# Modulation vectors summed along the free axis, a first mixer input built chunk by chunk, and angle tables moved into the first MLP

## The chip, the cores and the metric

The kernel runs on one core of one Trainium2 chip. A core has five engines with a queue each: PE (TensorE, matmuls), DVE (VectorE), ACT (ScalarE), POOL (GpSimd) and SP (SyncE, which here issues nearly all DMAs). Tensors live in SBUF with 128 partitions; PE sums into PSUM, eight banks of 128x512 fp32. The metric is the device time of one execution in microseconds (us), the median of several; lower is better.

## What is computed

Two stacks of two layers each over 512 tokens of width 1024, in fp32. A layer of the first stack is two sandwiches, a mixer and an MLP. Each has a modulation of its own, worked out from one vector c:

```python
def sandwich(x, c_act, sublayer, g_pre, g_post, w_mod, b_mod):
    shift, scale, gate = jnp.split(c_act @ w_mod + b_mod, 3, axis=-1)
    h = rms_norm(x, g_pre) * (1 + scale[:, None]) + shift[:, None]
    return x + gate[:, None] * rms_norm(sublayer(h), g_post)

def first_block(x, c, ...):
    c_act = jax.nn.silu(c)
    for layer in range(2):
        mixer = even_mixer if layer % 2 == 0 else odd_mixer
        x = sandwich(x, c_act, mixer, ...)
        x = sandwich(x, c_act, squared_relu_mlp, ...)
    return x
```

So there are 2 x 2 x 3 = 12 modulation vectors of 1024 numbers, each a product of c_act with a 1024x1024 matrix (4 MB). The even mixer (layer 0) projects `h` to the queries, keys and values of eight differential attention heads and to the inputs of a state-space part (SSD); the odd mixer (layer 1) is a retention beside a windowed attention. The second stack has gated delta, sparse and stick-breaking attention, a convolutional FFN, and an embedding added to the residual as `h + gate * rmsnorm(p[i] @ w_ple[i], ple_norm[i])`. Its rotary attention needs cosines and sines of `positions * inv`.

## The kernel before, in words

Activations stand transposed: eight chunks `x[k]` of 128 channels by 512 tokens. The kernel is written with a tile framework: the program gives the order of work, and a scheduler orders each engine's queue by the program's order (`high_priority(400)` moves a block ahead) and puts in the waits.

A projection's fp32 weights come in units of 128x1024 (512 KB). `wunit` (line 400) loads one (`wraw`, three buffers `wr`), rounds it on ACT into `whi` (`L409`), and takes the rest `wlo` on DVE (`L411`), or on GpSimd with `side=True`; `whi` and `wlo` have three buffers each. The activations are split likewise into `hh` and `hl`. `mm3` does three matmuls (hi by hi, lo by hi, hi by lo: `L418` to `L420`), 512 columns each, for every 128x128 block. `fm` gives outputs with features on partitions; `tm` (lines 452 to 466) gives tokens on partitions, in two passes of 256 columns (`L463` to `L465`), and is used for the values. `lead` starts two units at once, in the PSUM banks `s`.

Modulation: a step (`mod_step`, line 567) loads 128 rows of a matrix, multiplies them by 128 numbers of c_act, one to a partition, and adds to an accumulator (`mod_add`, `L583` and `L585`, 128x1024). After eight steps `mod_end` sums over the partitions by eight fp32 matmuls with a column of ones (`L592`; each is two records in the trace), and adds the bias. The steps of later vectors stand in a queue `modq`: `wunit` takes one per weight unit, unless `hold` says to let some units pass first.

The start (line 1943 on): the angle tables (`rope_tables`, two sines with two switches of ACT's function table), the loads of x, c_act from eight columns (`setup_c`), the statistic of x (`x_rstd`, eight squares `L332` on ACT, eight fp32 matmuls `L321`). `first_mod` makes the first two vectors, in halves of 512 outputs: five of eight row blocks go through PE with the column of c_act as the stationary side (`L619`), three through DVE. `pre_mod` then scales the eight chunks and splits them; for the first mixer its products `x[k] * r` are on GpSimd (`L657`). `even_mixer` begins with `diff_attention`: the leads of the first head's query and key units, and then, for each two heads, two value units by `tm` and the queries, keys, scores, softmax and values of the heads. `L802` is the scores' bias and row minimum in one pass, `L813` and `L817` are the transposes and the product with the values. The SSD part follows, then the output projection.

A statistic `Stat` squares on ACT (`L332`) and sums on PE (`L321`); with `side` set, the first `side` squares are summed on GpSimd (`L334`) and go to PE as one. `post_mod_` (line 666) normalises and adds to the residual (`L672`, `L673`, then the split `L482`); `ple_values` (line 1885) projects the embeddings of a layer, with its rests and its statistic on GpSimd, and stands at the end of MLP 0 and of the odd mixer.

Of the kernel before, what the change touches and what calls it, by code (L numbers as in the profile page):

```python
# [14 lines left out]
T = 512  # L15
# [20 lines left out]
def _tm_units(w):  # L36

    k, f = w.shape
    w = w.reshape(2, 4, 128, f // 256, 256).transpose(3, 0, 2, 1, 4)
    return np.ascontiguousarray(w.reshape(-1, 128, 1024))  # L40
# [146 lines left out]
def layout(inp):  # L187
# [4 lines left out]
    mw = g["mod_w"].reshape(4, 8, 128, 3, 1024).transpose(0, 3, 1, 2, 4)  # L192
# [3 lines left out]
    a["e_v"] = _tm_units(w[:, V:V + 1024])  # L196
# [58 lines left out]
    v.append(("c", _cols(g["c"][0])))  # L255
# [86 lines left out]
class Build:  # L342
# [218 lines left out]
    def setup_c(self):  # L561
        nc = self.nc
        self.cact = self.vp.tile([128, 8], F32, name="cact")
        e = self.sigmoid(self.vp, self.V("c"), tag="csg")
        nc.vector.tensor_mul(self.cact, e, self.V("c"))

    def mod_step(self, l, s, part, k):


        nc = self.nc  # L570
        if k == 0:
            self.macc = self.vp.tile([128, 1024], F32, tag="macc", name="macc", bufs=1)
        w = self.wr.tile([128, 1024], F32, tag="wr", name="mw")
        nc.sync.dma_start(w, self.ins["modw"][((l * 2 + s) * 3 + part) * 8 + k])
        self.mod_add(self.macc, w, k)
        if k == 7:
            self.mods[l, s, part] = self.mod_end(l, s, part, self.macc, slice(0, 8))

    def mod_add(self, acc, w, k, c=None):
        c = k if c is None else c  # L580
        col = self.cact[:, c:c + 1]
        if k == 0:
            self.nc.vector.tensor_scalar(acc, w, col, None, MUL)  # L583
        else:
            self.nc.vector.scalar_tensor_tensor(acc, w, col, acc, MUL, ADD)  # L585

    def mod_end(self, l, s, part, acc, ks):
        nc = self.nc
        ps = self.bank("t")
        n = ks.stop - ks.start  # L590
# [11 lines left out]
    def first_mod(self, pool):  # L602

        nc = self.nc
        ms = {}
        n = 512
        for i in range(2):
            for part in (1, 0):
                acc = pool.tile([128, n], F32, tag="macc", name="macc", bufs=4)
                ps = self.bank("d")  # L610
                first = [True, True]
                for k in range(8):
                    w = pool.tile([128, n], F32, tag="mw", name="mw", bufs=28)
                    nc.sync.dma_start(w, self.ins["modw"][8 * part + k][:, n * i:n * i + n])
                    if k in (2,4,6,):
                        self.mod_add(acc, w, 0 if first[1] else k, k)
                        first[1] = False
                    else:
                        nc.tensor.matmul(ps[0:1, 0:n], self.cact[:, k:k + 1], w, start=first[0], stop=False)  # L619
                        first[0] = False  # L620
                nc.tensor.matmul(ps[0:1, 0:n], self.C("ones")[:, 0:1], acc, start=False, stop=True)
                row = pool.tile([1, n], F32, tag="mrow", name="mrow", bufs=2)
                nc.vector.tensor_copy(row, ps[0:1, 0:n])
# [1309 lines left out]
def program(tc, ins, out, vat, phases=("mix0", "mlp0", "mix1", "mlp1", "b0", "b1", "fin")):  # L1933
    with ExitStack() as ctx:
# [3 lines left out]
        with ExitStack() as c1:  # L1938
# [6 lines left out]
            if first:  # L1945
                b.setup_c()
# [58 lines left out]
```

## Time and profile before

| | us |
|---|---|
| median of 3 runs | 3418.83 |
| lowest, highest | 3412.20, 3424.08 |
| the profiled execution | 3426.16 |
| its span (first to last instruction) | 3424.4 |
| PE busy in it | 3280.0 |
| DVE, ACT, POOL busy | 2216.6, 1690.6, 294.3 |
| mean granted TensorE clock | 0.982 of full speed |

A profile is one execution taken by the hardware profiler. A row of it gives the line of the program, the engine, the operation, and what is written from what. Matmuls are pipelined, so the busy times of neighbouring ones overlap; the distance from start to start is what one costs in a full stream. A wait is put down to the instruction that released it.

### The profile page before, as it was taken

The numbers are of one execution on the slowest core, as the hardware profiler recorded it, in microseconds if no ns is written. First come the engines' busy times: TensorE is split into PE (matmuls) and PEld (weight loads), VectorE is DVE, ScalarE is ACT, GpSimd is POOL, SyncE is SP. The second block draws the span as 40 slices with busy tenths as digits, with TensorE's granted clock in tenths as the row PEclk, the third lists the DMA queues.
The fourth block names the chain that finished last, engine by engine and source line by source line (L and its number), as shares of the span: only waits on it lengthen the run. The fifth ranks groups of instructions, "written<-read, shape, count | busy, mean of one in ns | idle before, by whom it ended". The sixth has DMA issues, their size and how long they took to land. (4 is left out here: it accounts for less than half of the span.)

```text
span 3424.4 us, 45576 instructions
## 1 busy us (share of the span) xinstructions
PE 3280.0 (96%) x17752; PEld 2580.1 (75%) x17752; DVE 2216.6 (65%) x3650; ACT 1690.6 (49%) x2922; POOL 294.3 (9%) x204
## 2 busy tenths in 40 slices
PE   8999998999989998999899999999989999999997
PEld 4877775888768776888667777888877777788885
DVE  6678775544486555444566766776776776587676
ACT  4666554323374335222355657544455565654445
POOL 2000111000110012000201002000030110200002
PEclk9999999999999999999989999999999999999998
DMA  7343222532333442232221002322322100222322
GB/s 260 117 146 116 68 74 73 172 113 93 106 108 117 148 136 95 93 98 93 83 74 62 26 31 77 99 96 95 99 89 75 62 26 22 80 96 95 99 93 77
DMA packets 97112, 323.93 MB, mean 95 GB/s; under 512 B 10936, under 2 KB 12472, under 8 KB 96768
## 3 DMA queue, kind: packets, MB, share of 16 engines
q1 hardware_dynamic: 96160, 319.44, 28.5%
q8 instruction: 140, 2.29, 0.3%
q10 hardware_dynamic: 576, 1.05, 0.1%
q14 instruction: 76, 0.62, 0.1%
q0 software_dynamic: 160, 0.52, 0.0%
HBM read 313.61 MB, written 9.98 MB: 94 GB/s over the span
## 5 line engine op out<-in xcount | busy, mean ns | idle before, releaser
L409 ACT CAST whi<-wr 128x1024 fp32r<-128x1024 f32 x459 | 480.3, 1048 | 867.1 <-PE pss L419 421.7
L411 DVE TENSOR_TENSOR wlo<-wr,whi 128x1024 fp32r<-128x1024 f32 x409 | 501.6, 1228 | 373.3 <-ACT whi L409 371.2
L418 PE MATMUL psg<-hh,whi 128*128 128x512 f32 x1448 | 584.3, 404 | 7.7 <-DVE gu L837 7.4
L420 PE MATMUL psg<-hh,wlo 128*128 128x512 f32 x1448 | 577.0, 398 | 0.0
L419 PE MATMUL psg<-hl,whi 128*128 128x512 f32 x1448 | 576.6, 398 | 0.0
L418 PE MATMUL pss<-hh,whi 128*128 128x512 f32 x784 | 310.6, 399 | 30.9 <-ACT hh L475 11.1
L418 PEld LDWEIGHTS psg<-hh,whi 128*128 128x128 f32 x1448 | 274.4, 190 | 67.1 <-issue 6.4
L420 PEld LDWEIGHTS psg<-hh,wlo 128*128 128x128 f32 x1448 | 273.4, 189 | 58.7 <-issue 5.8
L419 PEld LDWEIGHTS psg<-hl,whi 128*128 128x128 f32 x1448 | 273.7, 189 | 57.7 <-issue 7.4
L419 PE MATMUL pss<-hl,whi 128*128 128x512 f32 x784 | 312.3, 398 | 3.2 <-DVE hl L482 3.2
L420 PE MATMUL pss<-hh,wlo 128*128 128x512 f32 x784 | 311.0, 397 | 0.0
L334 POOL TENSOR_TENSOR sqacc<-sqacc,sq 128x512 f32<-128x512 f32 x86 | 126.5, 1471 | 1690.7 <-ACT sq L332 1689.9
L418 PE MATMUL psg<-mh,whi 128*128 128x512 f32 x560 | 223.9, 400 | 1.4 <-DVE x L680 1.3
L420 PE MATMUL psg<-mh,wlo 128*128 128x512 f32 x560 | 220.7, 395 | 0.0
L419 PE MATMUL psg<-ml,whi 128*128 128x512 f32 x560 | 220.1, 394 | 0.0
L418 PEld LDWEIGHTS pss<-hh,whi 128*128 128x128 f32 x784 | 150.2, 192 | 70.0 <-ACT hh L475 15.7
L419 PEld LDWEIGHTS pss<-hl,whi 128*128 128x128 f32 x784 | 151.1, 193 | 38.0 <-DVE hl L482 4.6
L420 PEld LDWEIGHTS pss<-hh,wlo 128*128 128x128 f32 x784 | 150.8, 192 | 34.0 <-issue 2.0
L411 POOL TENSOR_TENSOR wlo<-wr,whi 128x1024 fp32r<-128x1024 f32 x50 | 122.6, 2452 | 616.4 <-ACT whi L409 593.7
L418 PE MATMUL pss<-mh,whi 128*128 128x512 f32 x432 | 171.1, 396 | 0.5 <-DVE x L680 0.5
L420 PE MATMUL pss<-mh,wlo 128*128 128x512 f32 x432 | 169.7, 393 | 0.0
L419 PE MATMUL pss<-ml,whi 128*128 128x512 f32 x432 | 169.6, 392 | 0.0
(628 smaller groups left out, 6318.3 us busy)
## 6 DMA issues: line engine op xcount, KB each, us to landing
wr<-w SPq DMA_DIRECT2D x128, 512.0 KB, 3.5
wr<-up SPq DMA_DIRECT2D x88, 512.0 KB, 3.5
mw<-modw SPq DMA_DIRECT2D x80, 512.0 KB, 3.5
wr<-in SPq DMA_DIRECT2D x48, 512.0 KB, 3.5
wr<-down SPq DMA_DIRECT2D x40, 512.0 KB, 3.4
wr<-e_ssd SPq DMA_DIRECT2D x24, 512.0 KB, 3.5
wr<-e_qk SPq DMA_DIRECT2D x16, 512.0 KB, 4.1
mw<-modw SPq DMA_DIRECT2D x32, 256.0 KB, 5.4
```

The lines of the kernel that those rows point to most:

```text
L334: nc.gpsimd.tensor_add(self.acc, self.acc, sq)
L409: self.nc.scalar.copy(hi, raw)
L411: eng.tensor_sub(lo, raw, hi.bitcast(F32))
L418: mm(ps, ws[0], xs[0], start=first, stop=False)
L419: mm(ps, ws[0], xs[1], start=False, stop=False)
L420: mm(ps, ws[1], xs[0], start=False, stop=last)
```

## The change

The first mixer's input and its values are made chunk by chunk in `first_chunks`. Each of the eight channel chunks k takes its own 128 outputs of the scale and of the shift: the modulation weights are stored transposed, outputs on partitions, and `tensor_tensor_reduce` multiplies a 128x1024 tile by c_act (now a row of 1024, the same on all partitions) and sums along the row, starting at the bias, into one column. The chunk is scaled and split, and its 24 matmuls of the value projection go at once into all eight PSUM banks, 512 columns each. The value units are stored for that in another order (`_tw_units`); `diff_attention` copies the finished values out at its start and has neither value units nor leads. All other modulation vectors are summed in the same way, with no matmul and no accumulator. The angle tables are made in MLP 0 after the third group's first half, in the buffers `pt` of its activations. Three statistics that were summed on GpSimd are summed on PE (both embeddings' and the one after MLP 1), and the embeddings' rests are taken on DVE. The first mixer's products `x[k] * r` go from GpSimd to DVE, and `hold` is 12 there instead of 4.

```diff
     def mod_step(self, l, s, part, k):
         if k == 0:
-            self.macc = self.vp.tile([128, 1024], F32, tag="macc", name="macc", bufs=1)
+            self.mcol = self.vp.tile([128, 8], F32, name=f"mod{l}{s}{part}")
         w = self.wr.tile([128, 1024], F32, tag="wr", name="mw")
         nc.sync.dma_start(w, self.ins["modw"][((l * 2 + s) * 3 + part) * 8 + k])
-        self.mod_add(self.macc, w, k)
+        self.mod_dot(l, s, part, k, w, self.mcol[:, k:k + 1])
...
+    def mod_dot(self, l, s, part, k, w, col):
+        b = 8 * part + k
+        self.nc.vector.tensor_tensor_reduce(w, w, self.cact, 1.0, self.V(f"mb{l}{s}")[:, b:b + 1], MUL, ADD, col)
...
-        for j in range(n):
-            nc.tensor.matmul(ps[:, j:j + 1], acc[:, 128 * j:128 * j + 128], self.C("ones")[0:acc.shape[0], :1], start=True, stop=True)
-        m = self.vp.tile([128, n], F32, name=f"mod{l}{s}{part}{ks.start}")
-        nc.vector.tensor_add(m, ps[:, :n], self.V(f"mb{l}{s}")[:, 8 * part + ks.start:8 * part + ks.stop])
...
+    def setup_c(self, pool):
+        self.cact = self.vp.tile([128, D], F32, name="cact")
+        nc.sync.dma_start(self.cact, self.ins["crow"].to_broadcast([128, D]))
+        e = self.sigmoid(pool, self.cact, tag="mw", bufs=14)
+        nc.vector.tensor_mul(self.cact, e, self.cact)
...
+    def first_chunks(self, pool):
+        r = self.first_rstd
+        self.hold = 12
+        hs, ws = [], {}
+        acc = [[self.pg.tile([128, T], F32, tag="g", name="psg") if b < 2 and u == 0 else
+                self.bank("ggdd"[b] if u == 0 else "ssto"[b]) for b in range(4)] for u in range(2)]
+        for k in range(KC):
+            if k % 2 == 0:
+                ws = [self.wunit("e_v", k + u, 2) for u in range(2)]
+            cols = []
+            for part in (1, 0):
+                w = pool.tile([128, D], F32, tag="mw", name="mw", bufs=14)
+                nc.sync.dma_start(w, self.ins["modw"][8 * part + k])
+                m = self.vp.tile([128, 1], F32, name=f"mod00{part}{k}")
+                self.mod_dot(0, 0, part, k, w, m)
+                cols.append(self.mod_end(0, 0, part, m, slice(k, k + 1)))
+            t = self.nb.tile([128, T], F32, tag="pt", name="pt", bufs=3)
+            nc.vector.tensor_mul(t, self.x[k], r)
+            nc.scalar.activation(t, t, ACTF.Identity, scale=cols[0], bias=cols[1])
+            h = self.split(self.hp, "h", t)
+            hs.append(h)
+            for (hi, lo), pss in zip(ws, acc):
+                for b, ps in enumerate(pss):
+                    s = slice(128 * b, 128 * b + 128)
+                    mm = nc.tensor.matmul
+                    mm(ps, h[0][:, s], hi[:, k % 2], start=k == 0, stop=False)
+                    mm(ps, h[0][:, s], lo[:, k % 2], start=False, stop=False)
+                    mm(ps, h[1][:, s], hi[:, k % 2], start=False, stop=k == KC - 1)
+        return hs, acc
...
     def post_mod_(self, y, st, g, name):
-        self.xstat = Stat(self, KC, 7 if name else 0)
+        self.xstat = Stat(self, KC)
...
     def mlp(self, l, hs):
+                if g == 2 and l == 0:
+                    self.rope_tables()
...
     def diff_attention(self, hs, acc, p, outs):
+        v = p.tile([128, 4, D], F32, name="v")
+        for u in range(2):
+            for b in range(4):
+                nc.scalar.copy(v[:, b, T * u:T * u + T], acc[u][b])
-        self.lead("e_qk", (0, 1), hs)
         for u in range(4):
-            v = p.tile([128, 4, 256], F32, tag="v", name="v", bufs=2)
-            for b, ps in self.tm("e_v", u, hs):
-                nc.scalar.copy(v[:, 2 * b:2 * b + 2], ps)
...
     def ple_split(self, l, p):
-            self.nc.gpsimd.tensor_sub(lo, pt[:, k], hi.bitcast(F32))
+            self.nc.vector.tensor_sub(lo, pt[:, k], hi.bitcast(F32))
...
     def ple_values(self, l, p, hs):
-        st = Stat(self, KC, KC, tag="o", pool=p)
+        st = Stat(self, KC, tag="o", pool=p)
-            for j, ps in self.fm(f"ple_{l}", u, hs, side=True):
+            for j, ps in self.fm(f"ple_{l}", u, hs):
...
-            b.rope_tables()
-            b.load_x()
-            b.setup_c()
-            b.first_rstd = b.x_rstd(True)
...
                         with b.scope("mod0") as pm:
-                            b.first_mod(pm)
+                            b.setup_c(pm)
+                            b.load_x()
                             b.t5_tables()
-                            hs = b.pre_mod(0, 0, pm)
+                            b.first_rstd = b.x_rstd(True)
+                            hs, acc = b.first_chunks(pm)
```

## Rows read from the trace of the kernel before

**Rows 1.** Page, part 1: each engine's busy us, share of span, instructions

```profile
PE 3280.0 (96%) x17752; PEld 2580.1 (75%) x17752; DVE 2216.6 (65%) x3650; ACT 1690.6 (49%) x2922; POOL 294.3 (9%) x204
```

**Rows 2.** Windows: busy us of PE, PEld, DVE, ACT, POOL; clock; DMA; GB/s

```profile
0.00:10.00 10.00, 1.32 (x2) 0.81 (x3) 3.71 (x18) 4.00 (x8) 0.20 (x4) 1.00 0.67 227
10.00:20.00 10.00, 9.45 (x18) 3.42 (x18) 4.22 (x10) 9.10 (x13) 1.35 (x3) 1.00 1.05 361
```

**Rows 3.** Groups, 0-60 us: xcount | busy us, mean ns | idle before, releasers

```profile
L619 PE MATMUL psd<-mw,cact 128*1 128x512 f32 x40 | 19.9, 607 | 1.0 <-DMA mw<-modw 1.0
L418 PE MATMUL pss<-hh,whi 128*128 128x512 f32 x11 | 4.2, 412 | 0.0
L332 ACT ACTIVATE sq<-x 128x512 f32<-128x512 f32 x8 | 4.8, 625 | 3.3 <-DMA x<-xT 2.4 <-PE pst L321 0.8
```

**Rows 4.** Timeline of the start: start us, us, engine, line, operation [idle before]

```profile
23.21 0.68 DVE L532 SCALAR_TENSOR_TENSOR ry<-ry 128x512 f32<-128x512 f32 x1
40.26 1.52 ACT L658 ACTIVATE pt<-pt,mod,mod 128x512 f32<-128x512 f32 x2 [16.73 <-DVE mod L594]
```

**Rows 5.** Timeline, PE: first and last of two unbroken runs, narrow and wide

```profile
65.66 0.28 PE L465 MATMUL psg<-whi,hl 128*128 128x256 f32 x1
...
68.90 0.28 PE L465 MATMUL psg<-whi,hl 128*128 128x256 f32 x1
...
222.26 0.39 PE L418 MATMUL psg<-hh,whi 128*128 128x512 f32 x1
...
234.30 0.39 PE L420 MATMUL psg<-hh,wlo 128*128 128x512 f32 x1
```

**Rows 6.** Groups, 60-290 us, DVE; the last is a group of the page

```profile
L411 DVE TENSOR_TENSOR wlo<-wr,whi 128x1024 fp32r<-128x1024 f32 x27 | 33.0, 1222 | 26.5 <-ACT whi L409 26.4
L585 DVE SCALAR_TENSOR_TENSOR macc<-mw,cact,macc 128x1024 f32<-128x1024 f32 x22 | 28.2, 1280 | 5.5 <-DMA mw<-modw 5.4
L802 DVE CUSTOM_DVE_ANT_0 l<-pss,tt 128x512 f32<-128x512 f32 x16 | 10.9, 688 | 1.7 <-PE pss L519 0.8 <-PE psd L813 0.6
L802 DVE DVE_READ_ACCUMULATOR2_ANT sm<- 128x1 f32 x64 | 5.3, 83 | 0.0
L409 ACT CAST whi<-wr 128x1024 fp32r<-128x1024 f32 x459 | 480.3, 1048 | 867.1 <-PE pss L419 421.7
```

**Rows 7.** Windows of the attention, the SSD's beginning and MLP 0

```profile
60.00:270.00 210.00, 204.49 (x1186) 169.88 (x1186) 151.99 (x355) 136.35 (x291) 0.00 (x0) 1.00 0.42 135
290.00:350.00 60.00, 58.24 (x297) 44.82 (x296) 50.21 (x77) 32.35 (x51) 6.60 (x3) 1.00 0.46 148
600.00:940.00 340.00, 339.58 (x1481) 274.25 (x1479) 166.30 (x192) 105.68 (x135) 14.61 (x9) 1.00 0.37 120
```

**Rows 8.** Timeline, PE: one modulation vector's sixteen column products, and what follows

```profile
151.55 1.84 PE L592 MATMUL pst<-const,macc 128*128 128x1 f32 x16
153.25 0.36 PE L463 MATMUL psg<-whi,hh 128*128 128x256 f32 x1
```

**Rows 9.** Timeline, PE: first scores of two heads in succession

```profile
234.66 0.39 PE L518 MATMUL pss<-kt,qt 128*128 128x256 f32 x1
...
251.27 0.39 PE L518 MATMUL pss<-kt,qt 128*128 128x256 f32 x1 [0.40 <-ACT kt L508]
```

**Rows 10.** Post-modulation of MLP 0: a DVE group, and the window

```profile
L673 DVE SCALAR_TENSOR_TENSOR x<-y,mod,x 128x512 f32<-128x512 f32 x8 | 9.8, 1260 | 0.0
944.00:973.00 29.00, 18.54 (x50) 9.49 (x49) 23.04 (x25) 17.20 (x30) 12.61 (x8) 0.84 0.29 106
```

**Rows 11.** The same group in the odd mixer (1290 to 1316 us)

```profile
L672 DVE TENSOR_TENSOR y<-y,ry 128x512 f32<-128x512 f32 x8 | 10.5, 1356 | 0.0
```

**Rows 12.** Timeline after MLP 1, DVE, while GpSimd is idle

```profile
1685.97 1.29 DVE L672 TENSOR_TENSOR y<-y,ry 128x512 f32<-128x512 f32 x2
1687.19 1.41 DVE L673 SCALAR_TENSOR_TENSOR x<-y,mod,x 128x512 f32<-128x512 f32 x2
```

**Rows 13.** Waits of PE: us in total, times, longest us

```profile
PE pso L321 <- POOL sqacc L334: 8.5, 2, 4.5
```

More of the change, by code (lines that the diff above doesn't have):

```diff
@@ L600, in mod_end @@
         return m
-    def first_mod(self, pool):
+    def first_chunks(self, pool):
         nc = self.nc
-        ms = {}
-        n = 512
-        for i in range(2):
-            for part in (1, 0):
[L609 to L623, printed above, removed]
-                ms[part, i] = self.mod_end(0, 0, part, row, slice(n // 128 * i, n // 128 * (i + 1)))
-        for part in range(2):
-            self.mods[0, 0, part] = [ms[part, i] for i in range(2)]
@@ L655, in pre_mod_ @@
         for k in range(KC):
-            t = pool.tile([128, T], F32, tag="pt", name="pt", bufs=bufs)
-            mul.tensor_mul(t, self.x[k], r)
-            nc.scalar.activation(t, t, ACTF.Identity, scale=at(a, k), bias=at(shift, k))
+            t = self.nb.tile([128, T], F32, tag="pt", name="pt", bufs=3)
+            nc.vector.tensor_mul(t, self.x[k], r)
+            nc.scalar.activation(t, t, ACTF.Identity, scale=a[:, k:k + 1], bias=shift[:, k:k + 1])
             hs.append(self.split(self.hp, "h", t))
@@ L816, in diff_attention @@
                     for j in range(i + 1):
-                        nc.tensor.matmul(av[:, 128 * i:128 * i + 128], v[:, j, 128 * hh:128 * hh + 128], pt[:, j],
+                        nc.tensor.matmul(av[:, 128 * i:128 * i + 128], v[:, j, 128 * h:128 * h + 128], pt[:, j],
                                          start=j == 0, stop=j == i)
@@ new lines, in rope_tables @@
+        tile_ = lambda name, dt=F32: self.nb.tile([128, T], dt, tag="pt", name=name, bufs=3)
+        pi = tile_("posi", I32)
+        nc.sync.dma_start(pi, self.ins["pos"][0:1].to_broadcast([128, T]))
+        ang = tile_("ang")
+        nc.vector.tensor_copy(ang, pi)
+        n = tile_("angn")
+        nc.vector.tensor_scalar(ang, ang, self.C("inv64"), None, MUL)
+        nc.vector.tensor_scalar(n, ang, float(np.float32(0.5 / np.pi)), None, MUL)
+        nc.vector.tensor_scalar(n, n, MAGIC, None, ADD)
@@ new lines, in rope_tables @@
+        nc.vector.tensor_scalar(n, n, -MAGIC, None, ADD)
+        rest = 2 * np.pi
+        for bits in (8, 10, 24):
+            m, ex = np.frexp(rest)
+            c = float(np.float32(np.ldexp(np.round(np.ldexp(m, bits)), int(ex) - bits)))
+            rest -= c
+            nc.vector.scalar_tensor_tensor(ang, n, -c, ang, MUL, ADD)
+        nc.vector.tensor_scalar(ang, ang, 3.1415925, -3.1415925, MIN, MAX)
+        sn = tile_("angs")
+        with self.tc.manual_schedule(engines={mybir.EngineType.Activation}):
+            nc.scalar.activation(sn, ang, ACTF.Sin)
+            nc.scalar.activation(n, ang, ACTF.Sin, scale=0.5)
+            nc.scalar.preload_act_table_set("natural_log_exp_and_others")
@@ L1268, in head_norm @@
+        nc.vector.tensor_mul(n, n, n)
+        nc.vector.tensor_scalar(n, n, -2.0, 1.0, MUL, ADD)
+        nc.gpsimd.dma_start(self.dsin, sn)
+        nc.gpsimd.dma_start(self.dcos, n)
     def head_norm(self, o, col, tag="t"):
@@ L1960, in program @@
                         b.t5_rows()
-                    (b.even_mixer if l == 0 else b.odd_mixer)(hs)
+                    if l == 0:
+                        b.even_mixer(hs, acc)
+                    else:
+                        b.odd_mixer(hs)
                 if f"mlp{l}" in phases:
```

73 lines of the change are left out of this document (17 added, 56 removed).

## The prediction

> **What bounds the kernel now.** I began with the busy times of the page [rows 1]: PE is busy 96% of the span, DVE 65%, GpSimd 9%. So two things alone can move the end: PE work that goes, and stretches in which PE does nothing that counts. The windows then show where those stretches are. From 60 us on PE is nearly full: in the attention it idles 5.5 of 210 us, in MLP 0 0.4 of 340 [rows 7]. The large hole is the start. PE counts as busy there, but the groups say with what [rows 3]: forty passes of `L619` over the modulation weights, while the projections' matmuls (hi by hi `L418`, with two groups of the same kind beside it of 11 and 10) come to 32 by 60 us. From 10 us on the DMA engines are saturated at 361 GB/s [rows 2]: the 8.4 MB of the first two modulation matrices come in. The input's statistic is done at 23.9 us, and the first scaled chunk has to wait for the modulation until 40.3 us, 16.7 us of idle ACT [rows 4]. The order of reading was: busy times, windows, groups of the hole, timeline of its chain.
>
> The smaller holes are the post-modulations. After MLP 0 PE is busy 18.5 of 29 us at a granted clock of 0.84 [rows 10].
>
> **Prices.** In an unbroken run a 512-column matmul starts every 12.04/53 = 0.227 us, a 256-column one every 3.24/27 = 0.120 us (54 and 28 rows from first to last) [rows 5]. A DVE pass over 128x512 takes 0.65 to 0.70 us while GpSimd rests [rows 12], over 128x1024 with two tensor sources 1.22 to 1.28 us [rows 6].
>
> The new sum has no row of its form. The nearest is the attention's `L802`, a combined pass and reduction of the same kind (add and minimum) over 512 columns with one source in PSUM: 0.688 us, and 0.083 us to read its accumulator [rows 6]. With 512 columns more at the pace of `L411` I take 1.22 + 0.08 = 1.30 us; the bounds are 1.22 (reading costs nothing) and 2.44 us (half the rate). I take the low value because `L411` and `L585`, with both sources in SBUF, run at the full rate.
>
> [...]
>
> **The start.** Before: the 32 projection matmuls are worth 32 x 0.227 = 7.3 us, so 60.0 - 7.3 = 52.7 us of the start do no projection work. After: the first chunk needs the statistic and two sums. Ahead of chunk 0's second weight tile SP queues the constants, the vectors, the broadcast of c, x, the bucket table and two value units: 5.4 MB with the two tiles. At 2.3 MB in the first 10 us and 361 GB/s then [rows 2] that is 10 + 8.6 = 18.6 us; two sums make 21.2. The statistic loses the sines ahead of its last squares but gains four ACT passes over 1024 columns at 1.05 us [rows 6] for c's sigmoid beside eight squares of 0.63 us [rows 3]; I take 21 us (19 to 25). Then product 0.65, scaling 0.76 (1.52 for two [rows 4]) and cast with hand-overs 0.9: first matmul at 23.4 us.
>
> Each chunk is 24 matmuls of 512 columns, 24 x 0.227 = 5.45 us, eight of them 43.6 us. DVE per chunk: two sums 2.60, two column operations 0.2, product and rest 1.30, one weight rest on average 1.22: 5.3 us, just under PE. The data of chunk 7 is 16.0 MB in all, landed at 10 + 13.7/0.361 = 48 us, before PE reaches it at 61.5 us. So PE sets the pace, with little to spare. The new waits: SP, with three raw buffers, holds value unit 3 until unit 0 is split, and the modulation tiles of chunks 2 and 3 stand behind it; that is early. The three split buffers are tighter: the splits of units 3, 5 and 7 wait until PE is through the first half of the odd chunk before, and behind them on ACT and DVE, in program order, stand the next chunk's sums and scaling. That tail (cast 1.05, rest 1.22, sums 2.6, column operations 0.2, product 0.65, scaling and cast 1.4) is 7.1 us against the half chunk of 2.7 us that is left: up to 4.4 us three times, 13 us, if nothing is ordered ahead; nothing if the sums are. The modulation steps of before are ordered into gaps, they wait for DMA alone [rows 6], so I take about a third of it, and with a slow clock at the first matmuls add 6 us; bounds 0 to 20. The values are done at 23.4 + 43.6 + 6 = 73 us. Before, the same values cost 384 x 0.120 = 46.1 us of PE. Hence 73 - 46.1 = 26.9 us are lost instead of 52.7: **25.8 us gained** (12 to 32).
>
> Then all eight PSUM banks are full; ACT empties the first while PE finishes the last, so I put the handover at nothing; it costs 0.6 us a bank if the order is bad.
>
> **Column products gone.** Each of the ten later vectors loses sixteen PE records that hold PE 153.25 - 151.55 = 1.70 us [rows 8], 17.0 us. Nearly all lie where PE is full; **16 us gained** (12 to 17). The step itself stays on DVE at 1.30 instead of 1.28 us.
>
> **Attention without the value units.** They were filler. PE keeps 204.5 - 46.1 - 3 x 1.7 = 153 us of work; DVE loses eight weight rests (9.8) and eight modulation steps (10.2), since twelve units are now held back and not four: 152.0 - 20 = 132 us, 86% of PE's. In the beginning of the SSD part, at 84% DVE, PE idles 1.8 of 60 us [rows 7]. The chain from one head's first score to the next is 16.6 us, with that DVE load [rows 9]; PE needs 153/8 = 19.2, so PE still bounds. Idle grows from 5.5 to 7.5: **2 us lost** (-2 to 11). The eight steps land on the SSD part: **2 us lost** (0 to 5).
>
> **Off GpSimd.** While GpSimd works, DVE slows: eight `L673` take 9.8 us after MLP 0 and eight `L672` 10.5 in the odd mixer, against 0.70 and 0.65 each at rest, so 5.6 and 5.2 [rows 10 to 12]. That frees 4 to 5 us on the chain of each by that group alone, and the wait for the last GpSimd sum, 8.5 us for two [rows 13]. Against it each of the three statistics gives PE seven more fp32 products, at most 1.0 us each by `L619` [rows 3], 7 us. After MLP 0 PE has 10.5 us of idle for them [rows 10]; after MLP 1 it is fed as DVE goes, and they cost what they free. The lead units' rests stay on GpSimd, so part of the slowdown stays. I take -3, -3 and 0: **6 us gained** (18 gained to 12 lost). The embeddings' rests on DVE, 1.22 us each, lie in MLP 0, where DVE is half idle [rows 7].
>
> **Angle tables in MLP 0.** ACT is busy 31% and DVE 49% there [rows 7]; the tables take three of the buffers that the activations use, and two table switches on ACT stand ahead of PSUM evictions. Their load joins SP's queue of weights, their two stores GpSimd's empty one. **1 us lost** (0 to 4); without cover it is the sines and switches, some 4 us.
>
> **The sum.** -25.8 - 16 + 2 + 2 - 6 + 1 = -42.8 us. The profiled execution was 3426.2 us with a span of 3424.4; its own after would be 3383. It lies 7.3 us above the median of the three runs, 3418.8, against which I forecast 3377 (rounded up from 3376).
>
> **Rivals.**
> First: the sum with its accumulator runs at half rate, 2.44 us. For: no row shows the form. Against: the full rate of its neighbours. Then a chunk costs DVE 7.6 us, more than PE's 5.45: 8 x 2.15 less a head start of 2, 15 us; twelve steps put the attention's DVE at 146 of 153, 7 us; twenty steps put the SSD part over 95%, 9 us. 3377 + 31 = 3408.
> Second: the cover was needed. The chunk loop takes its whole 20 us of stalls (14 more), and each head idles the 1.6 us and more that PE shows where no value unit helps (about 8 more in all): 3399. For: DVE within 3% of PE per chunk. Against: the 16.6 us of a head.
> Third, the slower one: the same sum on DVE, but at a third of the rate or worse, 3.6 us. A chunk is then 9.9 us (33 lost), the attention's DVE 160 of 153 (20), the SSD part +46 us on DVE (35), the odd mixer 15: 3480. It is slower than before from about 2.7 us per sum. Against: every two-source row.
> Fourth: the start is bound by DMA, and nothing is gained there. Against: 48 us for the last tile when PE needs it at 61.5. I give it no weight of its own; it lies in the first terms' bounds.
>
> **How the numbers follow.** Forecast as above 0.69, own range 3354 to 3398; second rival 0.13; first 0.14; third 0.04. The range reaches to the first rival: 3354 to 3408. A measurement of this kernel can tell about 0.3%, 10 us: faster is under 3408.6. Of the first rival half lies below that, of the forecast and the second nearly all: faster 0.87, same 0.08, slower 0.05.
>
> **What would show it.** The first `L418`-like matmul of the values near 23 us and the last near 73; the sum at 1.22 us and its accumulator read at 0.08; PE idle under 10 us in the attention; no column products; the post-modulations' DVE passes back at 0.65 to 0.70 with PE's products in its gaps; MLP 0 still full. A sum above 2 us, PE waiting for DVE in each chunk, or idle between heads would make the prediction wrong.

## The result and the profile of the changed kernel

The changed kernel takes 3368.4 us (median; 3365.4 to 3369.2), the kernel before beside it 3420.4: 52 us less, a ratio of 0.985 with a 95% interval of 0.983 to 0.987. I had forecast 3377, with a range of 3354 to 3408. The profiled execution of the changed kernel took 3365.4 us with a span of 3363.6; between the two profiled executions lie 60.8 us. The medians differ by less, because the one of before lies above its median and the one of after below its own; where the surplus sits is shown further down.

Page of the changed kernel: the busy lines of PE, DVE and GpSimd, and the group of the new sum ([rows 1] of before; columns of the last line: busy us, mean ns, idle before it):

```profile
PE 3231.5 (96%) x17360; PEld 2540.6 (76%) x17360; DVE 2219.3 (66%) x3762; ACT 1693.6 (50%) x2922; POOL 232.8 (7%) x166
L591 DVE CUSTOM_DVE_ANT_0 mw<-mw,cact,vecs 128x1024 f32<-128x1024 f32 x96 | 123.3, 1287 | 56.2 <-DMA mw<-modw 55.8
```

The sum, which had no row before, is there: 96 of them at 1.287 us, and when DVE idles ahead of one it waits for the weights, not for another engine.

Timeline of the start, in place of the one in [rows 4] (start us, us, engine, line):

```profile
18.05 0.35 SPq L756 DMA_DIRECT2D t5d<-t5row  x1
19.00 2.36 DVE L419 TENSOR_TENSOR wlo<-wr,whi 128x1024 fp32r<-128x1024 f32 x2 [3.90 <-ACT whi L417]
20.53 0.63 ACT L535 ACTIVATE ry<-ry 128x512 f32<-128x512 f32 x1
21.27 0.68 DVE L538 SCALAR_TENSOR_TENSOR ry<-pst,ry 128x512 f32<-128x512 f32 x1
21.88 1.28 DVE L591 CUSTOM_DVE_ANT_0 mw<-mw,cact,vecs 128x1024 f32<-128x1024 f32 x1
23.08 0.08 DVE L591 DVE_READ_ACCUMULATOR2_ANT mod<- 128x1 f32 x1
23.08 0.69 DVE L539 TENSOR_TENSOR ry<-ry 128x512 f32<-128x512 f32 x1
23.74 1.28 DVE L591 CUSTOM_DVE_ANT_0 mw<-mw,cact,vecs 128x1024 f32<-128x1024 f32 x1
24.94 0.69 DVE L540 SCALAR_TENSOR_TENSOR ry<-ry 128x512 f32<-128x512 f32 x1
26.82 0.69 DVE L622 TENSOR_TENSOR pt<-x,ry 128x512 f32<-128x512 f32 x1
28.39 0.62 ACT L483 CAST hh<-pt 128x512 fp32r<-128x512 f32 x1
29.06 0.79 PE L630 MATMUL psg<-whi,hh 128*128 128x512 f32 x1 [10.14 <-ACT hh L483]
```

and of PE, two matmuls that follow one another early in the chunk loop, and its end:

```profile
36.53 0.63 PE L630 MATMUL pss<-whi,hh 128*128 128x512 f32 x1
36.95 0.54 PE L631 MATMUL pss<-wlo,hh 128*128 128x512 f32 x1
...
76.79 0.39 PE L632 MATMUL pso<-whi,hl 128*128 128x512 f32 x1
77.02 0.39 PE L426 MATMUL psg<-hh,whi 128*128 128x512 f32 x1
```

PE begins the values at 29.06 us and ends them at 77.0; up to 37 us, at a granted clock of 0.50, it starts most matmuls 0.43 us apart (ten steps from 32.26 us on take 4.27), and from then on, at 1.00, one every 0.227. Where the tables below need points in time, they are the first or last instruction of a line in the two traces:

| point, us | before | changed |
| --- | --- | --- |
| last product of the attention | 270.3 | 244.9 |
| first ReLU of MLP 0 | 589.3 | 564.9 |
| last ReLU of MLP 1 | 1657.9 | 1610.2 |
| levels copied, where the second stack begins | 1708.0 | 1654.7 |
| end | 3424.4 | 3363.6 |

So 24.4 us are gained by the start, the attention and the SSD part, 23.3 between the MLPs' ReLUs, 5.6 behind MLP 1, and 7.5 in the second stack, which the change does not touch. Windows of the changed kernel: attention, SSD part, and the post-modulation behind MLP 0 (columns as in [rows 2], [rows 7] and [rows 10]):

```profile
77.00:245.00 168.00, 162.29 (x809) 124.13 (x808) 136.31 (x356) 123.85 (x276) 0.00 (x0) 1.00 0.39 127
245.00:565.00 320.00, 296.58 (x1380) 224.24 (x1379) 241.05 (x385) 174.76 (x272) 41.03 (x22) 0.96 0.28 91
919.00:950.00 31.00, 27.43 (x86) 15.08 (x85) 22.87 (x32) 23.72 (x41) 3.17 (x1) 1.00 0.20 70
```

PE idles 5.7 us in the attention. Behind MLP 0 it is busy 27.4 of 31 us at full clock, where it was busy 18.5 of 29 at 0.84 [rows 10].

### The profile page after: what moved, and what is told of

The parts are those of the page before. It is cut to its first block, busy times and chain, and to the rows that moved or that the text cites. A ratio compares the mean times of both kernels' runs of the same rounds, so it can differ in the third digit from the quotient of the medians.

```text
span 3363.6 us, 44791 instructions
## 1 busy us (share of the span) xinstructions
PE 3231.5 (96%) x17360; PEld 2540.6 (76%) x17360; DVE 2219.3 (66%) x3762; ACT 1693.6 (50%) x2922; POOL 232.8 (7%) x166
## 5 line engine op out<-in xcount | busy, mean ns | idle before, releaser
L427 PE MATMUL pss<-hl,whi 128*128 128x512 f32 x768 | 304.2, 396 | 1.8 <-DVE hl L490 0.9
L428 PE MATMUL pss<-hh,wlo 128*128 128x512 f32 x768 | 303.0, 395 | 0.0
L342 POOL TENSOR_TENSOR sqacc<-sqacc,sq 128x512 f32<-128x512 f32 x66 | 96.1, 1456 | 1819.4 <-ACT sq L340 1819.0
L591 DVE CUSTOM_DVE_ANT_0 mw<-mw,cact,vecs 128x1024 f32<-128x1024 f32 x96 | 123.3, 1287 | 56.2 <-DMA mw<-modw 55.8
```

The lines of the kernel that those rows point to most:

```text
L342: nc.gpsimd.tensor_add(self.acc, self.acc, sq)
L427: mm(ps, ws[0], xs[1], start=False, stop=False)
L428: mm(ps, ws[1], xs[0], start=False, stop=last)
L591: self.nc.vector.tensor_tensor_reduce(w, w, self.cact, 1.0, self.V(f"mb{l}{s}")[:, b:b + 1], MUL, ADD, col)
```

## The experiments

All times are medians; the ratio is to the kernel before on the same chip, with its 95% interval. The kernel before took 3420.4 us beside the changed kernel of the first row, 3421.2 beside the first four experiments, 3421.7 beside the next four, 3421.5 beside the next three and 3424.2 beside the last.

| kernel | us | ratio |
| --- | --- | --- |
| changed | 3368.4 | 0.9850 (0.9830 to 0.9869) |
| later sums alone | 3405.6 | 0.9963 (0.9947 to 0.9978) |
| changed, GpSimd part undone | 3384.5 | 0.9906 (0.9891 to 0.9921) |
| changed, GpSimd works beside | 3391.8 | 0.9918 (0.9905 to 0.9932) |
| changed, angle tables first | 3376.1 | 0.9876 (0.9861 to 0.9892) |
| changed, no chunk order | 3391.8 | 0.9907 (0.9893 to 0.9922) |
| changed, other start order | 3373.4 | 0.9851 (0.9836 to 0.9866) |
| changed, twenty products at the start | 3374.8 | 0.9853 (0.9836 to 0.9869) |
| changed, both | 3368.6 | 0.9840 (0.9825 to 0.9855) |
| changed, start by hand | 3370.8 | 0.9860 (0.9841 to 0.9878) |
| changed, only the sums on GpSimd | 3381.2 | 0.9900 (0.9878 to 0.9921) |
| changed, a second pass per later sum | 3384.8 | 0.9899 (0.9881 to 0.9918) |
| changed, lead units' rests on DVE | 3359.4 | 0.9816 (0.9795 to 0.9836) |

### The later sums alone

```diff
         w = self.wr.tile([128, 1024], F32, tag="wr", name="mw")
-        self.mod_add(self.macc, w, k)
+        self.mod_dot(l, s, part, k, w, self.mcol[:, k:k + 1])
         if k == 7:
-            self.mods[l, s, part] = self.mod_end(l, s, part, self.macc, slice(0, 8))
+            self.mods[l, s, part] = self.mod_tail(l, s, part, self.mcol)
```

> The kernel before, with one part of the change alone: the eighty later modulation steps are sums along the free axis (the first two vectors stay as they were), so the ten sets of column products are gone. Added with it: one broadcast load of c and its sigmoid over 1024 columns, after the first chunks are scaled. By the prediction's term: 16 us gained (12 to 17), so about 3403 us beside 3419 of before. Rival, from the stage marks of the changed kernel, where attention, SSD and MLP 0 together gained nothing behind the start: the freed PE time is taken back by waits, and half or less is left, 3411 us or more. The sum should run at 1.28 us in the attention as well.

15.6 us less by the medians; by the ratio 13, between 8 and 18. At the levels the trace is 16.0 us ahead (1692.0 against 1708.0). The forecast term of 16 stands, and the rival (8 or less) lies at the edge of the interval: by the medians and at the levels nearly all of the 17.0 us of PE work that went is gained. The sum runs as fast here:

```profile
L590 DVE CUSTOM_DVE_ANT_0 mw<-mw,crow,vecs 128x1024 f32<-128x1024 f32 x80 | 102.5, 1281 | 62.6 <-DMA mw<-modw 61.9
```

### The GpSimd part: undone, beside, and the sums alone

```diff
-        self.xstat = Stat(self, KC)
+        self.xstat = Stat(self, KC, 7 if name else 0)
...
-        st = Stat(self, KC, tag="o", pool=p)
+        st = Stat(self, KC, KC, tag="o", pool=p)
...
-            for j, ps in self.fm(f"ple_{l}", u, hs):
+            for j, ps in self.fm(f"ple_{l}", u, hs, side=True):
```

with the embeddings' splits on `gpsimd` again. In the second kernel the sums of squares go to GpSimd as well, but PE keeps its products and GpSimd's result is not used; in the third only the two `Stat` lines are undone.

> The changed kernel with its GpSimd part undone: the embeddings' splits, weight rests and squares' sums, and the sums of the last post-modulation, are GpSimd's again; PE has seven products fewer for each of the three statistics. By the prediction's term: 6 us slower than the changed kernel (from 12 faster to 18 slower), 3374 us. Rival, from PE's lost time by stage in the two traces (10 us less behind MLP 0, 12 less from the odd mixer's end on, 5 less behind MLP 1): the part is worth about 27 us, 3395 us, and the granted clock falls again to half in the three post-modulations (before: 950 to 977 and 1243 to 1325 us; in the changed kernel only 1205 to 1208).

> The changed kernel, but GpSimd does its old work as well: the splits and weight rests of the embeddings are its own again, and it sums the squares of the three statistics beside PE, which keeps its seven added products for each; GpSimd's sums are not used. If the part is worth what it is because DVE no longer shares with GpSimd: as slow as with the part undone, whatever that is (3374 by my term, 3395 by the rival). If it is because PE has products to do where it had none, and so keeps its clock: as fast as the changed kernel, 3368 to 3373 us, with the clock at full speed in the post-modulations and DVE's passes there slow all the same (1.2 to 1.3 us instead of 0.7 to 1.0).

> The changed kernel with only the sums of squares of the three statistics back on GpSimd; the embeddings' splits and weight rests stay on DVE. With the whole GpSimd part undone the kernel took 3384.5 us, 16 more. If the sums carry it (GpSimd's seven adds of 1.4 us lie just where DVE does the passes of the post-modulation, and PE waits for the last of them): 3380 to 3385 us. Rival: the weight rests of the embeddings carry it (2.4 us each on GpSimd against 1.22 on DVE, and PE waits for them): 3370 to 3373 us.

Undone: 16.1 us slower than the changed kernel, and in the trace 18.3 us behind it at the levels. Beside: 23.4 us slower, though PE has all its products and waits for no GpSimd sum of these three statistics (the intervals of the two ratios overlap, so it is as slow as undone, as expected for that case). The sums alone: 12.8 us, most of it. So the gain is not PE's products and the clock they keep; it is that DVE is no longer held up. How it is held up is hidden by a mean; the same two lines with least, median and longest ns (behind MLP 0; changed kernel, then part undone):

```profile
L676 DVE TENSOR_TENSOR y<-y,ry x8: 679/684/694, 916.2 to 926.5; 128x512 f32<-128x512 f32 x8
L677 DVE SCALAR_TENSOR_TENSOR x<-y,mod,x x8: 740/744/2839, 917.4 to 927.7; 128x512 f32<-128x512 f32 x8
```

```profile
L676 DVE TENSOR_TENSOR y<-y,ry x8: 677/680/1792, 915.5 to 929.0; 128x512 f32<-128x512 f32 x8
L677 DVE SCALAR_TENSOR_TENSOR x<-y,mod,x x8: 737/740/2834, 917.8 to 930.2; 128x512 f32<-128x512 f32 x8
L342 POOL TENSOR_TENSOR sqacc<-sqacc,sq x9: 1274/1299/1761, 906.5 to 937.8; 128x512 f32<-128x512 f32 x9
```

Most passes are not slowed at all; a few stand still for 1.0 to 2.1 us, about as long as a GpSimd instruction (1.3 us an add, 2.4 a weight rest). Two of them, each with the GpSimd instruction that it meets (timeline with the part undone; start us, us):

```profile
915.62 1.70 POOL L342 TENSOR_TENSOR sqacc<-sqacc,sq 128x512 f32<-128x512 f32 x1 [3.53 <-ACT sq L340]
916.09 1.79 DVE L676 TENSOR_TENSOR y<-y,ry 128x512 f32<-128x512 f32 x1
924.54 1.43 POOL L342 TENSOR_TENSOR sqacc<-sqacc,sq 128x512 f32<-128x512 f32 x1 [0.25 <-ACT sq L340]
924.77 1.75 DVE L676 TENSOR_TENSOR y<-y,ry 128x512 f32<-128x512 f32 x1
```

In both, the pass ends 0.55 us after the GpSimd instruction has ended. From 80 us on in this trace, 80 DVE passes over 128x512 with both tensor sources in SBUF begin while GpSimd works, and 74 of them are held up (over 0.96 us); five of the other six begin in the last 0.33 us of GpSimd's instruction. Of 39 with one source in PSUM, none is held up. In the trace of the kernel before it is 73 of 79, which end 0.54 to 0.55 us after the GpSimd instruction that they meet, and none of 38. Why such a pass waits, no trace here shows.

With GpSimd beside, the same stage (columns: busy us, mean ns):

```profile
L682 DVE TENSOR_TENSOR y<-y,ry 128x512 f32<-128x512 f32 x8 | 9.3, 1204 | 0.0
L683 DVE SCALAR_TENSOR_TENSOR x<-y,mod,x 128x512 f32<-128x512 f32 x8 | 6.6, 868 | 0.0
L490 DVE TENSOR_TENSOR hl<-pt,hh 128x512 fp32r<-128x512 f32 x8 | 6.3, 823 | 1.2 <-ACT hh L489 1.2
L667 DVE TENSOR_TENSOR pt<-x,ry 128x512 f32<-128x512 f32 x8 | 6.0, 794 | 0.2
L546 DVE SCALAR_TENSOR_TENSOR ry<-ry 128x512 f32<-128x512 f32 x2 | 3.1, 1545 | 0.1
```

and in the changed kernel:

```profile
L677 DVE SCALAR_TENSOR_TENSOR x<-y,mod,x 128x512 f32<-128x512 f32 x8 | 7.7, 1006 | 0.0
L484 DVE TENSOR_TENSOR hl<-pt,hh 128x512 fp32r<-128x512 f32 x8 | 5.3, 687 | 2.3 <-ACT hh L483 2.3
L661 DVE TENSOR_TENSOR pt<-x,ry 128x512 f32<-128x512 f32 x8 | 5.2, 687 | 0.2
L676 DVE TENSOR_TENSOR y<-y,ry 128x512 f32<-128x512 f32 x8 | 5.1, 685 | 0.0
L540 DVE SCALAR_TENSOR_TENSOR ry<-ry 128x512 f32<-128x512 f32 x2 | 1.4, 692 | 0.1
```

31.3 us of DVE in place of 24.7 for the same passes: 6.6 us. The same can be counted over all of the stretch from the first ReLU of MLP 0 to the levels. A DVE pass counts as held up where it takes over 0.25 us more than the median of the same pass in the run with the lead units' rests on DVE (below), and the surplus is added up; every such pass meets a GpSimd instruction.

| kernel | held-up passes | surplus, us | the stretch, us |
| --- | --- | --- | --- |
| GpSimd beside | 24 | 25.1 | 1111.0 |
| GpSimd part undone | 21 | 23.4 | 1108.5 |
| only the sums on GpSimd | 20 | 22.5 | 1106.4 |
| changed | 2 | 4.2 | 1089.8 |
| lead units' rests on DVE | 0 | 0.0 | 1085.0 |

The stretch shortens by about what DVE no longer loses. With the part undone there is besides the wait that the change takes away ([rows 13] of before):

```profile
PE pso L329 <- POOL sqacc L342: 4.2, 1, 4.2
```

The granted clock in this stage is 1.00 in the changed kernel, 0.80 with the part undone and 0.89 with GpSimd beside, each over 31 us, and PE is busy 27.4, 22.5 and 24.5 us of them: it is lower where PE waits for DVE, with or without the added products. So in these runs it goes with the stall, and the products alone do not keep it up.

### Lead units' rests on DVE

```diff
     def lead(self, name, us, hs):
-        ws = [self.wunit(name, u, len(hs), side=True) for u in us]
+        ws = [self.wunit(name, u, len(hs)) for u in us]
```

> The changed kernel with one more thing off GpSimd: the weight rests of the two units that are made ready behind each norm (nine places, two units each). In the changed kernel one of them, 3.17 us on GpSimd, lies in the post-modulation behind MLP 0 and one in that of the odd mixer; the eight residual passes beside it take 1006 ns each, against 690 at rest, 2.5 us in all. If sharing with GpSimd alone sets the price: about 2 us gained at each of the places where DVE is on the chain, 3360 us or less. Rival: the two rests (1.22 us each on DVE) then stand in that chain themselves, 2.4 us in the place of 2.5, and the time is the same within 4 us, 3365 to 3373 us; slower than that if they are ordered ahead of the norm's passes.

3359.4 us (3358.2 to 3364.9), 9 less than the changed kernel by the medians; the two intervals still overlap a little, so it is at least as fast, and by the medians the fastest of all. The traces hold a part of it: from the first ReLU of MLP 0 to the levels this one takes 4.8 us less (table above), but it comes to that ReLU 4.6 us later, which I did not settle, and ends at 3363.1 us, level with the changed kernel's. Its profiled execution is the slowest of five, that of the changed kernel the fastest of four. The one long pass of the changed kernel (2839 ns above) is gone:

```profile
L677 DVE SCALAR_TENSOR_TENSOR x<-y,mod,x x8: 746/747/747, 921.4 to 929.6; 128x512 f32<-128x512 f32 x8
```

and the window of the stage (columns as above):

```profile
915.00:946.00 31.00, 29.92 (x97) 16.99 (x95) 24.86 (x38) 23.98 (x41) 0.00 (x0) 1.00 0.32 116
```

PE is busy 29.9 of the 31 us. The rests cost DVE 1.22 us each, but one runs ahead of the root (914.65 us, the root from 918.0) and one behind the last residual (930.3), not in the chain: my rival for this run did not hold.

### The chunk order and the tables

The first takes the accumulators out of `first_chunks` and puts the value units back into the attention, with the first sums kept:

```diff
-            for (hi, lo), pss in zip(ws, acc):
...
-        return hs, acc
+        return hs
...
         for u in range(4):
+            v = p.tile([128, 4, 256], F32, tag="v", name="v", bufs=2)
+            for b, ps in self.tm("e_v", u, hs):
+                nc.scalar.copy(v[:, 2 * b:2 * b + 2], ps)
```

The second has the angle tables at their old place:

```diff
-                if g == 2 and l == 0:
-                    self.rope_tables()
...
+            b.rope_tables()
             for l in range(2):
```

> The changed kernel with its first sums, but without the chunk order: the sixteen first sums and the eight scaled chunks are made as in the changed kernel, the value units stand in the attention again as pairs of two heads, each over all eight chunks, and no accumulators are held over the start. Tells whether the start is won by the sums (PE's forty passes over the weights gone) or by PE multiplying chunk by chunk while the weights still come in. If by the chunk order: DVE needs 4.3 us a chunk (two sums 2.7, column operations 0.2, two passes 1.4), the last chunk is scaled near 58 us, PE does 24 products (5.4 us) before and loses 52 us instead of 31; 21 us slower than the changed kernel less 2 for the filler in the attention, 3388 us. If by the sums: the chunks are scaled as the weights land, PE is in full work by 45 us, 3377 us or less.

> The changed kernel with the angle tables back at the very start, ahead of c, of x and of the statistic. By the prediction: MLP 0 gets 1 us back (0 to 4), and the start loses the two sines with their table switches ahead of the statistic, some 4 us: first value matmul at 33 us instead of 29.06, 3371 us in all. Rival: the statistic waits for x and for the sigmoid's passes anyhow, the tables fit beside it, and the time is that of the changed kernel or 1 us less, 3367 to 3368 us.

Without the chunk order 23.4 us are lost, close to the 20 of the first theory, and at the last product of the attention (274.6 us) the trace is even 4.3 us behind the kernel before: in this order of work the sums alone win nothing at the start. PE stands still (timelines of PE, SP and ACT, without the chunk order):

```profile
18.21 1.98 PE L329 MATMUL pst<-sq,const 128*128 128x512 f32 x4
51.77 0.80 PE L426 MATMUL pss<-hh,whi 128*128 128x512 f32 x1 [31.57 <-ACT whi L417]
38.91 0.34 SPq L405 DMA_DIRECT2D wr<-e_qk  x1
50.69 1.98 ACT L417 CAST whi<-wr 128x1024 fp32r<-128x1024 f32 x2
```

What ends the wait is not the last chunk but the cast of the first weights. Their load is issued at 38.9 us, where it was issued at 8.6 before, and their casts stand on ACT behind the work on all eight chunks. So the run changes the weights' place too, and the 23.4 us are the price of both; what the sums would win with the weights made ready early was not tried.

With the tables first the kernel is 7.7 us slower by the medians, though the two intervals overlap a little (4.8 at the levels of the trace). I had 3; they come ahead of the statistic, and the chunk loop begins 6.9 us later and ends 5.2 us later:

```profile
35.99 0.80 PE L630 MATMUL psg<-whi,hh 128*128 128x512 f32 x1 [10.77 <-ACT hh L483]
...
81.97 0.39 PE L632 MATMUL pso<-whi,hl 128*128 128x512 f32 x1
```

### Four tries at the start

Another order (`x_rstd` at high priority, the bucket tables first, two modulation tiles ahead of the value units); twenty added products that keep PE busy; both with ten; and DVE's order of the first two chunks fixed, the store of the bucket row on GpSimd's queue, and six products. The edits of the first, of the second and of the fourth; the third joins the first two:

```diff
...
+                            b.t5_tables()
                             b.setup_c(pm)
                             b.load_x()
-                            b.t5_tables()
-                            b.first_rstd = b.x_rstd(True)
+                            with tc.high_priority(400):
+                                b.first_rstd = b.x_rstd(True)
```

```diff
+        for k in range(20):
+            nc.tensor.matmul(acc[1][3], self.C("ones"), self.x[k % KC], start=True, stop=True)
         for k in range(KC):
             if k % 2 == 0:
```

```diff
...
+            if k < 2:
+                es.enter_context(self.tc.manual_schedule(engines={mybir.EngineType.DVE}))
...
+            if k == 0:
+                r = self.x_rstd(True)
...
-            nc.sync.dma_start(dr, row)
+            nc.gpsimd.dma_start(dr, row)
...
```

> The changed kernel with another order at the start alone: the bucket tables' work first, the statistic at high priority, and the first two modulation tiles loaded ahead of the value units. In the changed kernel two sums stand between the passes of the reciprocal root on DVE (21.27 to 25.6 us), and the first value matmul starts at 29.06 us where I had forecast 23.4. If that order is what came between: first value matmul at 24 to 25 us, and the end 4 to 5 us earlier, 3364 us. Rival: the chunk loop is fed at the pace of DVE, the earlier start is waited away before the last value matmul, and the time is that of the changed kernel, 3368 us.

> The changed kernel with twenty products added (ones times a chunk of x, into an accumulator's bank before its first use; the result is not used), placed on PE between the statistic's products and the first value matmul, where PE idles 10.1 us. In the changed kernel the granted clock is at half from 23.6 to 37.3 us, and the value matmuls of 29.06 to 37.3 us start every 0.43 us instead of 0.227. If the idle of before is why the clock falls: full clock from the first value matmul on, 8.2 us of matmuls in 4.1, the end 4 us earlier, 3364 us. Rival: the clock falls all the same, or the chunks are not scaled any faster, so that PE waits between them: 3368 us.

> The last two together, with ten added products in the shorter gap. If both causes hold and do not overlap: first value matmul at 24 to 25 us at full clock, last near 69 us, 8 us earlier than the changed kernel, 3360 us. Rival: from the first chunk on DVE's 5.3 us per chunk is the pace (PE needs 5.45), both gains meet there and no more than one of them is kept, 3364 us.

> The changed kernel with its start put in order by hand: the bucket tables' work first and their row's store on GpSimd's queue instead of SP's (in the changed kernel SP stands behind that store from 11.2 to 18.0 us), the first two modulation tiles loaded ahead of the value units, and DVE's instructions of the first two chunks in a fixed order, first sums, then the reciprocal root, then the first product, and only then the weights' rests. Six products of ones and x are added on PE behind the statistic (results not used) at 0.87 us each, as the run with twenty of them showed. If DVE's order and the clock are what made the start 4 us worse than forecast: first value matmul at 26 us at full clock, 0.227 us apart, last at 70 us instead of 76.8, and the levels of the second stack (1654.7 us in the changed kernel) 6 to 7 us earlier. Rival: with PE at full clock so early the weights or DVE (5.3 us a chunk beside PE's 5.45) no longer keep up, PE waits in the chunk loop, and the last value matmul comes at 72 us or later, as in the run with both edits (71.9).

The new order did not do what it was to do: the squares moved ahead of c's sigmoid, the first sum came at 20.3 us with the weights' rests still between the root's passes, and the first value matmul at 29.15. That run tells nothing about the order I meant.

The twenty products were mis-sized. One over 512 columns leaves two records and takes 0.87 us, not 0.43 (19 of them in the second row):

```profile
9.17 2.05 PE L612 MATMUL pso<-x,const 128*128 128x512 f32 x2 [9.17 <-DMA x<-xT]
19.70 16.47 PE L612 MATMUL pso<-x,const 128*128 128x512 f32 x38
35.61 0.80 PE L632 MATMUL psg<-whi,hh 128*128 128x512 f32 x1
79.34 0.39 PE L634 MATMUL pso<-whi,hl 128*128 128x512 f32 x1
```

They hold the first value matmul back by 6.6 us, yet the last comes only 2.6 later: at a granted clock of 1.00 (36 to 80 us) the loop is 4.0 us shorter, as expected. With both edits the values run from 28.45 to 72.1 us, by hand from 30.44 to 74.1, both 43.7 us, and 192 times 0.227 is 43.6: PE never waits in the loop. By hand the first matmul was not at 26 us, since the statistic itself ended later there, at 22.6 us instead of 18.9.

None of the four is measurably faster than the changed kernel. With both edits the trace is 7.5 us ahead at the first ReLU of MLP 0 and 4.0 at the levels; by hand 4.3 and then 1.2 behind. Where the rest goes in MLP 0 and the odd mixer I did not settle.

### A second pass for each later sum

```diff
+        nc.vector.tensor_tensor(w, w, w, mybir.AluOpType.max)
         self.mod_dot(l, s, part, k, w, self.mcol[:, k:k + 1])
```

> The changed kernel with one more pass over the whole tile ahead of each of the eighty later sums (the tile's maximum with itself, which changes nothing): about 1.22 us more of DVE for each step, 98 us in all, nothing else. This is the price of the first rival, a sum at half the rate, without its share at the start. By the rival's working: attention's DVE comes within 5% of PE (7 us), the SSD part over 95% (9 us), the rest is covered: 3368 + 16 = 3384 us. If DVE's slack covers it: 3370 us or less. If the steps lie on the chains of the post-modulations as well: 3390 us or more.

16.4 us slower, where the rival's working gave 16. The places differ: at the end of the attention the trace is 1.7 us behind and not 7, at the first ReLU of MLP 0 5.1 and at the levels 13.4. So the size came out by two errors that cancel; attention and SSD have more slack on DVE than I gave them, and the later stages, which I had called covered, have less.

## Why the prediction was right, and where it was not

| term | forecast | measured |
| --- | --- | --- |
| start | -25.8 (-32 to -12) | -21.8 |
| column products | -16 (-17 to -12) | -15.6; 16.0 at the levels |
| attention and SSD part | +4 (-2 to +16) | +4.2 |
| off GpSimd | -6 (-18 to +12) | -16.1; 18.3 at the levels |
| tables in MLP 0 | +1 (0 to 4) | not told apart |

The start is 77.0 - 46.1 = 30.9 us lost, by the forecast's own reckoning, against 52.7. For the attention and the SSD part: 24.4 us are gained at the first ReLU, of them 21.8 by the start, and four sets of column products (6.8) lie ahead of it, so 4.2 went back. At the levels the terms are -16.0 by the run with the later sums alone, -18.3 by the run with GpSimd undone, and what is left of the 53.3, -19.0, is start, attention, SSD part and tables, for which the forecast had -20.8. That the time came within 9 us of the forecast is in part luck: the start gained 4 us less than forecast and the GpSimd part 10 to 12 more.

*The start.* The step that failed is the first value matmul at 23.4 us; it came at 29.06. I had let the root be ready at 21 us, beside the two sums. Both are DVE's work, and from 19.0 us on DVE runs without a gap: two weight rests (2.4 us), the root's three passes and two sums between them, then a third sum, and the product starts at 26.8 instead of 21.2. I had priced each piece and not queued them on their engine. That this queue is the cause is read from the trace; no run isolates it, for the tries that changed DVE's order moved other things too and brought the first value matmul to 28.45 us at the earliest. The term for stalls was wrong the other way: the tail behind the split buffers never showed, since sums and scaling are ordered ahead; the slow clock that I had put into the same 6 us cost 4.0. Each error is smaller than its term's bounds, and they partly cancel.

*The sum.* Forecast 1.30 us with its read; measured 1.28 and 0.08. The half rate of the first rival (2.44 us) and the 3.6 us of the third were my estimates, and no run shows either: with two fp32 sources of 1024 columns in SBUF the sum took 1.287 us (mean of 96), and 1.281 (of 80) in the run with the later sums alone. First and third rival are gone with it. The rows that speak for the full rate were the neighbours of the same shape [rows 6].

*The cover.* The second rival is gone too: 5.7 us of idle PE in the attention, against 5.5 before [rows 7].

*Off GpSimd.* This is the mis-sized term, and the reason that the time is 9 us below the forecast. That DVE slows while GpSimd works was named and the rows were there [rows 10 to 13], but I set seven fp32 products for each statistic against it and let them eat the gain behind MLP 1. They take 0.87 us each and lie where PE waits anyhow, so I take it that they cost little; no run prices them by themselves. I also counted the slowdown of one group of passes in each stage, where it reaches nearly every DVE pass with two tensor sources in SBUF that begins while GpSimd works (74 of 80 above): the root, the products with it, the splits. Five groups make 6.6 us behind MLP 0.

*The tables.* At their old place they cost 7.7 us by the medians (5.2 in the chunk loop); I had put the sines at about 4 and MLP 0's share at 1, which no run separates from the rest.

*The second stack.* 7.5 of the 60.8 us between the two traces are not the change's. Windows of its first 52 us and of the rest: before, changed, later sums alone, GpSimd part undone.

```profile
1708.00:1760.00 52.00, 47.59 (x194) 33.21 (x193) 36.52 (x67) 25.95 (x46) 2.76 (x2) 0.80 0.20 72
1760.00:3424.00 1664.00, 1604.03 (x9885) 1272.18 (x9882) 1151.53 (x1954) 889.23 (x1588) 144.61 (x110) 0.99 0.23 74
```

```profile
1654.70:1706.70 52.00, 48.67 (x301) 36.13 (x300) 38.64 (x73) 30.17 (x57) 2.56 (x2) 1.00 0.21 72
1706.70:3363.00 1656.30, 1597.27 (x9802) 1267.82 (x9800) 1149.20 (x1948) 884.45 (x1577) 144.51 (x110) 0.99 0.23 75
```

```profile
1692.00:1744.00 52.00, 47.58 (x297) 34.88 (x295) 38.81 (x73) 30.80 (x58) 2.72 (x2) 0.97 0.22 73
```

```profile
1673.00:1725.00 52.00, 47.59 (x196) 33.25 (x195) 36.44 (x67) 25.94 (x46) 2.74 (x2) 0.80 0.21 71
```

From the levels to the end these four take 1716.4, 1708.9, 1706.7 and 1718.8 us. The two at a clock of 0.80 are the long ones, one with the change and one without; a kernel that leaves the second stack and the GpSimd part as before is the shortest. But that clock does not explain the difference: of all fourteen traces here four take 1706.7 to 1709.0 us and ten 1712.7 to 1718.9, and two of the ten (1715.4 without the chunk order, 1715.8 with the second pass) have a clock of 0.97 over those 52 us, as three of the four have. What does explain it is open.

## What to carry over

Cost the work on GpSimd by the DVE passes that meet it (here those with both tensor sources in SBUF, 1.0 to 2.1 us each), on every pass of the chain, and read a line's least, median and longest time before its mean; work taken off an engine that was 9% busy gave as much here as 17 us of PE work that went. Work put in front of the first matmul is to be queued on its engine, instruction by instruction, and not only priced. And where PE is full, what it no longer has to do is gained nearly one for one (here 15.6 to 16.0 of 17.0 us).

## What the hardware showed that I had not expected

- A fp32 product of 128x512 costs PE 0.87 us at a granted clock of 1.00 (19 of them took 16.47 us) and leaves two records, so the mean of a group (0.6 us for `L619` in [rows 3]) is not its price.
- At the start PE idles 10.1 us between the statistic and the first value matmul, and the granted clock is 0.66 over 20 to 40 us and 0.50 over 29 to 37: most of the first seventeen matmuls start 0.43 us apart, against 0.227 at 1.00. With products in the gap the clock was 1.00 throughout (19 to 80 us with twenty, 20 to 72 with both edits). The 4.0 us that this is worth did not show in the time.
- A DVE pass over 128x512 with both tensor sources in SBUF that began while GpSimd worked was held up in 74 of 80 cases with the part undone and in 73 of 79 before, and there it ended 0.54 to 0.55 us after GpSimd's instruction; one with a source in PSUM was not held up (none of 39 and of 38).
- The second stack, whose code no experiment but the last changes, took 1706.7 to 1718.9 us in the fourteen traces. A difference of 10 us between two single traces of this kernel says nothing about where the change is.
